# Gated linear attention by scores between all 256 tokens, without carried states

## The chip, the cores and the metric

The kernel runs on one core of a Trainium2 chip. The metric is the device time of one execution in microseconds (us); lower is better. TensorE (PE, with its weight loads listed as PEld), VectorE (DVE), ScalarE (ACT), GpSimd (POOL) and SyncE (SP, which issues nearly all transfers here) run side by side and wait for each other by semaphores. A difference of 0.3% of the time, some 3.6 us, is about the least that repeated runs tell from none.

## The reference, cut to what matters

One decoder layer for 256 tokens of width 1024: a modulation from a condition vector, one wide input projection whose columns feed all branches, a gated linear attention (GLA), a short convolution, gates and an output projection, and then a mixture of 64 experts. The part that changes is the attention:

```
def gla_chunked(q, k, v, log_a):                 # 4 heads, dk=128, dv=256, CHUNK=64
    b = jnp.cumsum(gc, axis=3)                   # within a chunk of 64 tokens
    q_t = qc * jnp.exp(b)
    k_t = kc * jnp.exp(-b)
    k_s = kc * jnp.exp(b_last - b)
    attn = jnp.where(causal, einsum(q_t, k_t), 0.0)
    o_intra = einsum(attn, vc)
    ...
    def step(state, inp):                        # over the 4 chunks
        o_i = q_i @ state
        state = d_i[..., None] * state + k_i.T @ v_i
```

After it each head's output is divided by its root mean square over the head's 256 values, scaled, and multiplied by silu(r).

## The kernel before, in words

The layer is done in two parts. The first part, up to about 300 us, works through 88 blocks of weights (`items`), 512 KB each, 24 matmuls or so a block. Blocks 0 to 15 are v and q/k, then come c (16 to 23), r (24 to 31), h (32 to 39), b, a, g, and the three output projections A, C and O. SP loads a block into a ring of 12 places; ACT rounds it to the short float format (`split_h`, L340), DVE forms the remainder (`split_l`, L347), which also frees the ring's place for the next load, and PE multiplies in three passes (`mm_blk`, L356). Splits run five blocks ahead of their matmuls (`LA`). Modulation weights come through the same ring, and DVE multiplies them with the condition (`mod_blk`, L257); the table `MODS` says beside which block each one stands.

The second part multiplies the experts' weights, 16 groups of 12 units of 2 MB each, with the tokens routed to them (L1020, L1048, L1075). `Stream` loads a unit whenever a piece of SBUF comes free; the first units are loaded while the first part still runs.

The order of the work is written by hand. The loop over blocks runs, for block `b`, first what is listed under `first(b, ..)`, then splits for a later block, then the evacuation of the block before, then `pre(b, ..)`, then the rest of the splits, then `at(b, ..)`, and then the block's matmuls. Each engine takes its own instructions in that order. The attention is such a list of steps between blocks 16 and 47:

- `gate0` to `gate8`: the forget gate, its sum over each chunk of 64 tokens (`bb`, the scan at L450), and the exponentials `eb`, `enb`, `ekb`.
- `k_evac`, `q_evac`: k and q leave PSUM times these exponentials, k twice (`ks` for the states, `kt_` for the scores).
- `gla_kst`, `gla_kst2` (block 27 and 28): `ks` transposed by PE (L481) and copied by ACT.
- `gla_attn`, `gla_attn2` (28 and 29): scores in two tiles of 128 by 128 tokens a head (L494), masked by DVE (L498) to two chunks each.
- `gla_state`, `gla_state2` (29 to 32): chunk by chunk k times v (L506, with 64 rows), and the running states S on ACT and DVE (L513, L515).
- `gla_o` (33 and 34): scores times v (L525) and states times q (L529), five matmuls for each of 8 halves of a head.
- `gla_ss` to `gla_ss4` (36 to 39): sums of squares by four column groups (L541), root, reciprocal, and the spread of each head's number to all 128 partitions by a matmul with a selection matrix `P1` (L556).

## Time and profile before

| | |
|---|---|
| median of 3 runs | 1206.16 us (1203.33 to 1206.17) |
| the profiled execution | 1202.4 us, of which the span from the first to the last instruction is 1200.5 us |
| PE / DVE / ACT busy | 903.8 / 381.6 / 224.6 us |
| moved by DMA | 477.84 MB, 398 GB/s over the span |

The span is read in stretches: "PE busy" is what PE did in one, "DMA share" is the mean busy share of the 16 DMA engines, and "PEclk" the clock that PE was granted, 1.00 being 2.4 GHz.

### The profile page before, as it was taken

Reading aid. Unit: us, or ns where it says so; the run is one execution under the profiler, and the core shown is the slowest. Engines: PE = TensorE matmul, PEld = TensorE weight load, DVE = VectorE, ACT = ScalarE, POOL = GpSimd, SP = SyncE. Lnnn points to the kernel's source line nnn. Section 1 sums busy time; section 2 is a strip of 40 time slices with the busy share of each in tenths; the row PEclk is TensorE's granted clock in tenths of the full one; section 3 lists DMA queues with packets and bytes.
Section 4 is the critical chain, followed back from the end, with each engine's and each line's share of the span. In section 5 each row is a group of like instructions: output and inputs, shape, how many; then the busy total and the mean of one; then the engine's idle time right before and its main releaser. Section 6 shows DMA issues by size and latency. Waiting matters only on the chain.

```text
span 1200.5 us, 14607 instructions
## 1 busy us (share of the span) xinstructions
PE 903.8 (75%) x6188; PEld 476.8 (40%) x6188; DVE 381.6 (32%) x720; ACT 224.6 (19%) x375; POOL 3.9 (0%) x15
## 2 busy tenths in 40 slices
PE   9999999999888766666666667676667566756575
PEld 6999999999342212121212212121212111412112
DVE  8968699664431111111111101020202000302103
ACT  6775545443210101010101000000000000100002
POOL 0000000000000000000000000000000000000000
PEclk9999999999998888798788888788888886989888
DMA  9987589979999999999999999999999999999996
GB/s 369 396 339 254 177 300 339 381 271 364 421 430 430 429 432 431 430 431 430 430 432 430 429 432 430 430 432 429 431 431 430 431 430 431 428 432 431 429 428 261
DMA packets 51483, 477.84 MB, mean 398 GB/s; under 512 B 5971, under 2 KB 6099, under 8 KB 27093
## 3 DMA queue, kind: packets, MB, share of 16 engines
q1 hardware_dynamic: 50544, 475.81, 95.8%
q8 instruction: 50, 0.82, 0.2%
q10 hardware_dynamic: 868, 1.05, 0.2%
q14 instruction: 21, 0.16, 0.0%
HBM read 475.79 MB, written 1.05 MB: 397 GB/s over the span
## 4 chain that ended last, share of the span: by engine, by line
DMA 67%; PE 28%; DVE 3%; ACT 0%; issue 0%; DVEq 0%; SPq 0%; ACTq 0%
DMA unit<-in_ew_dram 45%; DMA ring<-in_ew_dram 19%; PE z L356 17%; PE a L1048 3%; DMA unit<-in_el_dram 2%; PE m L364 2%; PE z L373 2%; PE m L1020 1%; PE m L1075 1%; PE m L529 0%; DMA xt<-in_xT_dram 0%; PE z L220 0%; PE m L506 0%; PE m L525 0%; PE m L312 0%
## 5 line engine op out<-in xcount | busy, mean ns | idle before, releaser
L1048 PE MATMUL a<-unit,xt 128*32 128x512 f32 x1440 | 209.5, 711 | 103.9 <-DMA unit<-in_ew_dram 103.9
L1048 PE MATMUL a<-unit,gt 128*32 128x512 f32 x736 | 121.7, 799 | 63.5 <-DMA unit<-in_ew_dram 59.9
L1048 PEld LDWEIGHTS a<-unit,xt 128*32 128x32 f32 x1440 | 43.8, 120 | 248.2 <-DMA unit<-in_ew_dram 139.0
L356 PE MATMUL z<-hhl,sp 128*128 128x256 f32 x1152 | 140.9, 284 | 0.0
L356 PEld LDWEIGHTS z<-hhl,sp 128*128 128x128 f32 x1152 | 138.9, 192 | 1.6 <-issue 1.5
L1024 ACT ACTIVATE xt<-m,modc,A 128x128 f32<-128x128 f32 x64 | 25.9, 453 | 518.5 <-PE m L1020 517.4
L347 DVE TENSOR_TENSOR sp<-ring,sp 128x1024 fp32r<-128x1024 f32 x88 | 106.8, 1219 | 40.2 <-ACT sp L340 40.1
L1048 PE MATMUL a<-ring,xt 128*32 128x512 f32 x608 | 84.2, 676 | 35.9 <-DMA ring<-in_ew_dram 35.9
L340 ACT CAST sp<-ring 128x1024 fp32r<-128x1024 f32 x88 | 91.5, 1048 | 93.8 <-PE z L356 66.6
L1079 DVE TENSOR_TENSOR wk<-wk,m 128x512 f32<-128x512 f32 (+2 forms) x64 | 41.7, 654 | 194.5 <-PE m L1075 194.5
L1066 DVE TENSOR_TENSOR xt<-a,xt 128x1024 f32<-128x1024 f32 (+3 forms) x19 | 20.0, 1054 | 257.4 <-PE a L1048 249.8
L1048 PEld LDWEIGHTS a<-unit,gt 128*32 128x32 f32 x736 | 24.3, 129 | 148.6 <-DMA unit<-in_ew_dram 93.1
L1075 PE MATMUL m<-xt,pwt 128*128 128x512 f32 (+2 forms) x136 | 64.5, 617 | 5.2 <-DVE xt L1066 5.2
L1056 DVE TENSOR_TENSOR gt<-gt,a 128x512 f32<-128x512 f32 x16 | 11.0, 687 | 173.8 <-ACT gt L1055 173.8
L1020 PEld LDWEIGHTS m<-scr,wk 128*128 128x128 f32 x512 | 58.7, 192 | 19.0 <-issue 18.7
L1020 PE MATMUL m<-scr,wk 128*128 128x128 f32 x512 | 62.4, 279 | 3.7 <-DVE scr L1009 2.9
L257 DVE SCALAR_TENSOR_TENSOR xt<-ring,xt 128x1024 f32<-128x1024 f32 x48 | 58.5, 1218 | 0.6 <-DMA ring<-in_modw_dram 0.2
L1048 PEld LDWEIGHTS a<-ring,xt 128*32 128x32 f32 x608 | 18.6, 117 | 97.3 <-DMA ring<-in_ew_dram 49.3
L1026 DVE TENSOR_SCALAR xt<-m,A,modc 128x128 f32<-128x128 f32 x64 | 23.3, 405 | 103.9 <-PE m L1020 103.9
L1048 PE MATMUL a<-ring,gt 128*32 128x512 f32 x208 | 36.3, 833 | 21.8 <-DMA ring<-in_ew_dram 21.1
L1075 PEld LDWEIGHTS m<-xt,pwt 128*128 128x128 f32 x136 | 26.0, 206 | 50.3 <-issue 38.0
L1055 ACT ACTIVATE gt<-a 128x512 f32<-128x512 f32 x16 | 9.6, 597 | 182.3 <-PE a L1048 182.3
(255 smaller groups left out, 633.0 us busy)
## 6 DMA issues: line engine op xcount, KB each, us to landing
unit<-in_ew_dram SPq DMA_DIRECT2D x136, 2048.0 KB, 38.8
ring<-in_ew_dram SPq DMA_DIRECT2D x48, 2048.0 KB, 38.8
ring<-in_win_dram SPq DMA_DIRECT2D x88, 512.0 KB, 7.8
ring<-in_modw_dram SPq DMA_DIRECT2D x48, 512.0 KB, 6.8
ring<-in_ew_dram SPq DMA_DIRECT2D x12, 512.0 KB, 7.3
unit<-in_el_dram SPq DMA_DIRECT2D x4, 1024.0 KB, 31.6
ring<-in_el_dram SPq DMA_DIRECT2D x4, 512.0 KB, 20.2
unit<-in_el_dram SPq DMA_DIRECT2D x4, 512.0 KB, 11.2
```

The lines of the kernel that those rows point to most:

```text
L257: V.scalar_tensor_tensor(scr, st.block("m", i, b), 1.0, cB, op0=OP.mult, op1=OP.mult, accum_out=modc[:, 4 * i + b:4 * i + b + 1])
L340: S.copy(sp(b)[:, 0], st.block("w", n, i))
L347: V.tensor_sub(t[:, 1], st.block("w", n, i), t[:, 0].bitcast(F32))
L356: T.matmul(ps, t[:, ws, k], rhs[rs][:, k], start=(clear and k == 0 and n == 0), stop=(k == KT - 1 and n == 2), skip_group_check=True)
L364: T.matmul(pb[:, h % 2], t[:, ws, h], hl[rs][:, kk], start=(kk == 0 and h % 2 == 0 and n == 0), stop=(kk == KT - 1 and h % 2 == 1 and n == ...
L373: T.matmul(pv[tt][hh], hl[rs][:, kk, 128 * tt:128 * tt + 128], t[:, ws, 512 * hh:512 * hh + 512], start=(kk == 0 and n == 0), stop=(kk == ...
L1020: T.matmul(ps[j], acc[:, tt, f:f + 128], Pm[:, tt], start=(tt == 0), stop=(tt == 1))
L1024: S.activation(xg[:, k], ps[j], AF.Identity, bias=B2[:, k:k + 1], scale=A2[:, k:k + 1])
L1026: V.tensor_scalar(xg[:, k], ps[j], A2[:, k:k + 1], B2[:, k:k + 1], op0=OP.mult, op1=OP.add)
L1048: T.matmul(ps[32 * j:32 * j + 32, 512 * hh:512 * hh + 512], lhsT[:, 32 * j:32 * j + 32], w[:, j, 512 * hh:512 * hh + 512], start=first, st ...
L1075: T.matmul(ps[:, :w], pwt[:, tt], X["y"][:, s], start=True, stop=True)
L1079: V.tensor_add(total[:, tt, s], total[:, tt, s], ps[:, :w])
```

## The change

The attention no longer carries states from chunk to chunk. The 256 tokens are taken as two tiles of 128. Inside a tile, the exponentials are measured from the end of the tile's first chunk: `wE` is the gate's sum at that end minus the running sum, and `eq` and `ek` get exponentials of plus and minus it (first chunk) and of the running sum (second chunk). One product of k and q then gives the scores of all pairs of a tile; the products of the first 64 tokens as keys are one matmul, those of the second 64 as keys, against the second 64 as queries alone, another (`gla_attn`, 64 rows of output each). For keys of tile 0 and queries of tile 1, `gla_far` multiplies k and q by the decay to the tile's edge, and a third product gives their scores. `gla_near` masks with a plain causal mask, `gla_cross` copies the third product, and `gla_o` needs two matmuls for each half of a head: 256 queries against the keys of tile 0, 128 against those of tile 1. Transposes, states and their copies are gone. The products stand at block 29, where those of the scores stood at block 28. The spread of the head norms takes one row of ones at partition 0, 32, 64 or 96 for each head, each into a PSUM tile of its own; `P1` is no longer filled at the start. Three entries of `MODS` move.

```diff
@@ -32,7 +32,7 @@
 FAR = 8192.0
 START = (2, 2, 0, 2, 8)
 XS = 38
-MODS = (16, 17, 18, 19, 22, 26, 27, 28, 31, 33, 34, 35, 37, 39, 41, 43, 45, 47, 49, 51, 52, 53, 54, 55, 56, 57, 58,
+MODS = (16, 17, 18, 19, 22, 26, 28, 29, 30, 33, 34, 35, 37, 39, 41, 43, 45, 47, 49, 51, 52, 53, 54, 55, 56, 57, 58,
         59, 60, 61, 62, 63)
 LA = 5
 SPLIT = ("T6", "T7", "T3")
@@ -229,7 +229,6 @@
     V.tensor_scalar(ident, jp, 0.0, None, op0=OP.is_equal)
     cmask = sm.tile([128, 128], I32, name="cmask")
     V.tensor_scalar(cmask, jp, 0.0, None, op0=OP.is_ge)
-    V.memset(cmask[0:64, 64:128], 0)
     tri = sm.tile([128, 128], BF, name="tri")
     V.tensor_scalar(tri, jp, 0.0, None, op0=OP.is_gt)
     trif = sm.tile([128, 128], BF, name="trif")
@@ -245,9 +244,6 @@
     G.memset(smask.rearrange("p (c t) -> p c t", t=64)[:, :, 0:1], 0.0)
 
     P1 = sm.tile([128, 2, TT, 128], F32, name="P1")
-    G.memset(P1, 0.0)
-    for h in range(H):
-        G.memset(P1[32 * h:32 * h + 1, h // 2, h % 2], 1.0)
     scr2 = sm.tile([128, 256], F32, name="scr2")
 
 
@@ -405,13 +401,19 @@
 
     t9 = big.tile([128, 4, 1024], F32, name="t9", tag="T9")
     gb = big.tile([128, 4, H, TOK], F32, name="gb", tag="T10")
-    la, bb, eb, enb = (t9[:, i].rearrange("p (h t) -> p h t", h=H) for i in range(4))
+    la, bb, eq, ek = (t9[:, i].rearrange("p (h t) -> p h t", h=H) for i in range(4))
     L["sr"], L["osq"] = (t9[:, 2 * i:2 * i + 2].rearrange("p a (k t) -> p (a k) t", t=TOK) for i in range(2))
     L["v"] = t8[:, 0].rearrange("p (t d) -> p t d", t=2)
     L["o"] = gb[:, 2:4].rearrange("p a h t -> p (a h) t")
-    ekb, qt, kt_, ks = (gb[:, i] for i in range(4))
-    decay = sm.tile([128, H, 4], F32, name="decay")
-    b4 = bb.rearrange("p h (c t) -> p (h c) t", t=64)
+    wE, qx, kx = gb[:, 0, 0:2].rearrange("p h t -> p (h t)"), gb[:, 1], gb[:, 3]
+    wE = wE.rearrange("p (a t) -> p a t", t=64)
+    kd, qd = (gb[:, 2].rearrange("p h t -> p (h t)")[:, 512 * i:512 * i + 512].rearrange("p (h t) -> p h t", h=H)
+              for i in range(2))
+    decay = sm.tile([128, 4, H], F32, name="decay")
+
+    def half(t, c):
+
+        return t.rearrange("p h (a c t) -> p (h a) c t", c=2, t=64)[:, :, c]
 
     def gate0():
         ps = zt(512)
@@ -450,84 +452,59 @@
         V.tensor_tensor_scan(fl(bb), smask, fl(la), 0.0, op0=OP.mult, op1=OP.add)
 
     def gate5():
-        S.activation(eb, bb, AF.Exp, scale=-1.0 / 16)
+
+        V.tensor_sub(wE, half(bb, 0)[:, :, 63:64].to_broadcast([128, 8, 64]), half(bb, 0))
 
     def gate6():
-        V.tensor_sub(ekb.rearrange("p h (c t) -> p (h c) t", t=64),
-                     b4[:, :, 63:64].to_broadcast([128, 16, 64]), b4)
-
-    def gate7():
-        V.tensor_copy(decay, eb.rearrange("p h (c t) -> p h c t", t=64)[:, :, :, 63])
-
-    def gate8():
-        S.activation(enb, bb, AF.Exp, scale=1.0 / 16)
-        S.activation(ekb, ekb, AF.Exp, scale=-1.0 / 16)
+        for d, sg in ((ek, -1.0), (eq, 1.0)):
+            S.activation(half(d, 0), wE, AF.Exp, scale=sg / 16)
+            S.activation(half(d, 1), half(bb, 1), AF.Exp, scale=-sg / 16)
+        for c in range(2):
+            S.activation(decay[:, c], bb[:, :, 64 * c + 127], AF.Exp, scale=-1.0 / 16)
 
 
 
     def gla_setup():
         g2 = big.tile([128, 4, 1024], F32, name="gc", tag="T11")
-        L["kst"] = g2[:, 0].rearrange("p (t d) -> p t d", t=2)
-        L["at"] = g2[:, 1].rearrange("p (t h i) -> p t h i", t=2, h=H)
-        for ch, i in ((1, 2), (2, 3), (3, 0)):
-            L["S", ch] = g2[:, i].rearrange("p (h d) -> p h d", h=H)
-        G.memset(g2[:, 1], 0.0)
-
-    def gla_kst():
-        L["pk"] = []
-        for tt in range(TT):
+        L["at0"] = g2[:, 0].rearrange("p (h i) -> p h i", h=H)
+        L["at1"] = g2[:, 1, 0:512].rearrange("p (h i) -> p h i", h=H)
+        G.memset(L["at0"][:, :, 0:128], 0.0)
+        G.memset(L["at1"], 0.0)
+
+    def gla_far():
+        for d, x, c, o in ((kd, kx, 0, 0), (qd, qx, 1, 128)):
+            V.tensor_mul(d, x[:, :, o:o + 128], decay[:, c, :, None].to_broadcast([128, H, 128]))
+
+    def gla_attn():
+        L["pa"] = []
+        a, b = slice(0, 128), slice(128, 256)
+        for k, q in ((kx[:, :, a], qx[:, :, a]), (kx[:, :, b], qx[:, :, b]), (kd, qd)):
             ps = mt(H, 128)
             for h in range(H):
-                T.transpose(ps[:, h], ks[:, h, 128 * tt:128 * tt + 128], ident)
-            L["pk"].append(ps)
-
-    def gla_kst2():
-        for tt in range(TT):
-            S.copy(L["kst"][:, tt], fl(L["pk"][tt]))
-
-    def gla_attn():
-        L["pa"] = []
-        for tt in range(TT):
-            s = slice(128 * tt, 128 * tt + 128)
-            ps = mt(H, 128)
-            for h in range(H):
-                T.matmul(ps[:, h], kt_[:, h, s], qt[:, h, s], start=True, stop=True)
+                if k is kd:
+                    T.matmul(ps[:, h], k[:, h], q[:, h], start=True, stop=True)
+                    continue
+                T.matmul(ps[0:64, h], k[:, h, 0:64], q[:, h], start=True, stop=True, skip_group_check=True)
+                T.matmul(ps[64:128, h, 64:128], k[:, h, 64:128], q[:, h, 64:128], start=True, stop=True,
+                         skip_group_check=True)
             L["pa"].append(ps)
 
-    def gla_attn2(tt):
-        V.copy_predicated(L["at"][:, tt], cmask[:, None, :].to_broadcast([128, H, 128]), L["pa"][tt])
-
-    def gla_state(*chs):
-        for ch in chs:
-            L["ps", ch] = [mt(2, 256) for _ in range(2)]
-        for h in range(H):
-            for ch in chs:
-                tt, r = ch // 2, slice(64 * (ch % 2), 64 * (ch % 2) + 64)
-                T.matmul(L["ps", ch][h // 2][:, h % 2], L["kst"][r, tt, 128 * h:128 * h + 128],
-                         L["v"][r, tt, 256 * h:256 * h + 256], start=True, stop=True)
-
-    def gla_state2(ch):
-        new = L["S", ch + 1]
-        for h in range(H):
-            if ch == 0:
-                S.copy(new[:, h], L["ps", ch][h // 2][:, h % 2])
-            else:
-                V.scalar_tensor_tensor(new[:, h], L["S", ch][:, h], decay[:, h, ch:ch + 1],
-                                       L["ps", ch][h // 2][:, h % 2], op0=OP.mult, op1=OP.add)
+    def gla_near(tt):
+        t, ps = (L["at0"][:, :, 0:128], L["at1"])[tt], L["pa"][tt]
+        for n, c in ((64, 0), (128, 64)):
+            V.copy_predicated(t[:n, :, c:c + 64], cmask[:n, None, c:c + 64].to_broadcast([n, H, 64]), ps[:n, :, c:c + 64])
+
+    def gla_cross():
+        S.copy(L["at0"][:, :, 128:256], L["pa"][2])
 
     def gla_o(h):
         ps = mt(2, TOK)
         vt = L["v"]
         for a in range(2):
             f = 256 * h + 128 * a
-            for tt in range(TT):
-                s = slice(128 * tt, 128 * tt + 128)
-                T.matmul(ps[:, a, s], vt[:, tt, f:f + 128], L["at"][:, tt, h],
-                         start=(a == 0 and tt == 0), stop=False, skip_group_check=True)
-            for ch in range(1, 4):
-                s = slice(64 * ch, 64 * ch + 64)
-                T.matmul(ps[:, a, s], L["S", ch][:, h, 128 * a:128 * a + 128], qt[:, h, s],
-                         start=False, stop=(a == 1 and ch == 3), skip_group_check=True)
+            T.matmul(ps[:, a], vt[:, 0, f:f + 128], L["at0"][:, h], start=(a == 0), stop=False, skip_group_check=True)
+            T.matmul(ps[:, a, 128:256], vt[:, 1, f:f + 128], L["at1"][:, h], start=False, stop=(a == 1),
+                     skip_group_check=True)
         L["po", h] = ps
 
     def gla_o2(h):
@@ -549,16 +526,15 @@
         V.reciprocal(scr2, scr2)
 
     def gla_ss4():
-        L["rso"] = []
+        L["rso"] = [mt(TOK) for _ in range(H)]
         for h in range(H):
-            if h % 2 == 0:
-                L["rso"].append(mt(2, TOK))
-            T.matmul(L["rso"][h // 2][:, h % 2], P1[:, h // 2, h % 2], scr2, start=True, stop=True)
+            r = slice(32 * h, 32 * h + 1)
+            T.matmul(L["rso"][h], onesf[r], scr2[r], start=True, stop=True)
 
     def o_norm(h):
         oT = L["o"]
         o = oT[:, 2 * h:2 * h + 2]
-        V.tensor_mul(o, o, L["rso"][h // 2][:, h % 2:h % 2 + 1].to_broadcast([128, 2, TOK]))
+        V.tensor_mul(o, o, L["rso"][h][:, None, :].to_broadcast([128, 2, TOK]))
         for k in (2 * h, 2 * h + 1):
             V.scalar_tensor_tensor(oT[:, k], oT[:, k], colt[:, CGG + k:CGG + k + 1], L["sr"][:, k],
                                    op0=OP.mult, op1=OP.mult)
@@ -611,25 +587,18 @@
     first(19, gate2)
     first(20, gate3)
     at(20, gate4)
-    at(21, gate6)
-    first(22, gate5)
-    first(23, gate8)
-    at(23, gate7)
+    at(21, gate5)
+    first(22, gate6)
     at(23, lambda: k_evac(0))
     at(24, lambda: k_evac(1))
     at(25, lambda: q_evac())
     at(25, gla_setup)
+    at(27, gla_far)
     at(40, st.free, "T12")
-    at(27, gla_kst)
-    at(28, gla_attn)
-    first(28, gla_kst2)
-    pre(29, gla_attn2, 0)
-    pre(29, gla_attn2, 1)
-    at(29, gla_state, 0, 1)
-    first(30, gla_state2, 0)
-    pre(30, gla_state2, 1)
-    at(31, gla_state, 2)
-    pre(32, gla_state2, 2)
+    at(29, gla_attn)
+    first(31, gla_cross)
+    pre(31, gla_near, 0)
+    pre(31, gla_near, 1)
     at(33, gla_o, 0)
     at(33, gla_o, 1)
     first(34, gla_o2, 0)
@@ -716,13 +685,12 @@
 
     def q_evac():
         for j in range(2):
-            V.scalar_tensor_tensor(qt[:, 2 * j:2 * j + 2], pq[j], 128.0 ** -0.5, eb[:, 2 * j:2 * j + 2],
+            V.scalar_tensor_tensor(qx[:, 2 * j:2 * j + 2], pq[j], 128.0 ** -0.5, eq[:, 2 * j:2 * j + 2],
                                    op0=OP.mult, op1=OP.mult)
 
     def k_evac(j):
         s = slice(2 * j, 2 * j + 2)
-        V.tensor_mul(ks[:, s], pk[j], ekb[:, s])
-        V.tensor_mul(kt_[:, s], pk[j], enb[:, s])
+        V.tensor_mul(kx[:, s], pk[j], ek[:, s])
 
     def b_evac(q, ps):
         if q == 0:
```

On PE, between blocks 26 and 34, stands before (L356 is the block's work, `gb` holds the scaled q and k, `gc` transposed k, scores and states, `t_126` v):

```order
L481 MATMUL m<-ident,gb 128x128 x8
L356 MATMUL z<-hhl,sp 128x256 x24
L494 MATMUL m<-gb 128x128 x8
L356 MATMUL z<-hhl,sp 128x256 x24
L506 MATMUL m<-t_126,gc 128x256 x8
L356 MATMUL z<-hhl,sp 128x256 x48
L506 MATMUL m<-t_126,gc 128x256 x4
L356 MATMUL z<-hhl,sp 128x256 x48
L525 MATMUL m<-gc,t_126 128x128 x2
L529 MATMUL m<-gb,gc 128x64 x3
```

And in the changed kernel, from the last pair of scores on (seven pairs like it stand ahead; L352 is the block's work there, `t_120` v):

```order
L487 MATMUL m<-gb 64x128
L488 MATMUL m<-gb 64x64
L485 MATMUL m<-gb 128x128 x4
L352 MATMUL z<-hhl,sp 128x256 x96
L505 MATMUL m<-gc,t_120 128x256
L506 MATMUL m<-gc,t_120 128x128
```

The transposes, both groups of state products and the three short matmuls of each half of a head have gone; all scores stand in one place, four blocks of work ahead of their use.

On DVE, from q's evacuation (L719) to the masks, stands before (`sp` are the split weights, `xt,modc` the modulation):

```order
L719 SCALAR_TENSOR_TENSOR gb<-m,t_181 128x512 x2
L347 TENSOR_TENSOR sp<-ring,sp 128x1024
L257 SCALAR_TENSOR_TENSOR xt,modc<-ring,xt 128x1024
L347 TENSOR_TENSOR sp<-ring,sp 128x1024
L257 SCALAR_TENSOR_TENSOR xt,modc<-ring,xt 128x1024
L347 TENSOR_TENSOR sp<-ring,sp 128x1024
L257 SCALAR_TENSOR_TENSOR xt,modc<-ring,xt 128x1024
L263 TENSOR_TENSOR modc<-modc,colt 128x4
L498 COPY_PREDICATED gc<-cmask,m 128x512 x2
```

And in the changed kernel (L688 is q's evacuation, L476 `gla_far`):

```order
L688 SCALAR_TENSOR_TENSOR gb<-m,t_175 128x512 x2
L343 TENSOR_TENSOR sp<-ring,sp 128x1024
L253 SCALAR_TENSOR_TENSOR xt,modc<-ring,xt 128x1024
L343 TENSOR_TENSOR sp<-ring,sp 128x1024
L476 TENSOR_TENSOR gb<-gb,decay 128x512 x2
L343 TENSOR_TENSOR sp<-ring,sp 128x1024
L253 SCALAR_TENSOR_TENSOR xt,modc<-ring,xt 128x1024
```

Behind q's evacuation now stand two splits and one modulation block, and then the two products that PE's third group of scores needs.

On ACT, at the exponentials, stands before (L453, L463 and L464 are the three exponentials, L715 copies c):

```order
L453 ACT_TABLE_LOAD
L453 ACTIVATE t_181<-t_181 128x1024
L340 CAST sp<-ring 128x1024
L715 COPY t_126<-z 128x512
L463 ACTIVATE t_181<-t_181 128x1024
L464 ACTIVATE gb<-gb 128x1024
L340 CAST sp<-ring 128x1024 x2
```

And in the changed kernel:

```order
L460 ACT_TABLE_LOAD
L460 ACTIVATE t_175<-gb 128x8x64
L461 ACTIVATE t_175<-t_175 128x8x64
L460 ACTIVATE t_175<-gb 128x8x64
L461 ACTIVATE t_175<-t_175 128x8x64
L463 ACTIVATE decay<-t_175 128x4 x2
L336 CAST sp<-ring 128x1024
L684 COPY t_120<-z 128x512
L336 CAST sp<-ring 128x1024 x2
```

All exponentials now stand ahead of the first of the three casts; before, two of the three stood behind it.

## Rows read from the trace of the kernel before

**Rows 1.** From the page: the span, and the chain of waits that ended last, as shares of the span by engine.

```profile
span 1200.5 us, 14607 instructions
...
DMA 67%; PE 28%; DVE 3%; ACT 0%; issue 0%; DVEq 0%; SPq 0%; ACTq 0%
```

**Rows 2.** Busy time by stretch: us from the span's start, its length, then busy us and instructions of PE, PEld, DVE, ACT and POOL, the granted clock of PE, the DMA share and GB/s.

```profile
94.60:149.70 55.10, 53.96 (x442) 51.24 (x441) 37.62 (x55) 26.18 (x39) 0.00 (x0) 1.00 0.66 211
149.70:240.00 90.30, 90.30 (x753) 90.27 (x752) 79.29 (x113) 42.77 (x51) 0.00 (x0) 1.00 0.92 339
...
300.00:374.00 74.00, 63.04 (x489) 26.74 (x491) 25.68 (x97) 15.36 (x36) 0.00 (x0) 0.95 1.00 425
374.00:1180.00 806.00, 533.95 (x3301) 164.18 (x3293) 116.69 (x255) 45.01 (x97) 0.00 (x0) 0.85 1.01 430
```

**Rows 3.** The same view in stretches of 5 us, three of those in which the DMA engines had gaps.

```profile
235.00:240.00 5.00, 5.00 (x44) 5.00 (x43) 2.65 (x3) 1.80 (x2) 0.00 (x0) 1.00 0.63 211
...
260.00:265.00 5.00, 5.00 (x44) 5.00 (x43) 2.44 (x5) 0.62 (x1) 0.00 (x0) 1.00 0.60 182
...
295.00:300.00 5.00, 4.95 (x22) 2.87 (x21) 4.00 (x25) 3.06 (x9) 0.00 (x0) 1.00 0.88 313
```

**Rows 4.** The chain of waits in order of time: start us, us, what ran or was waited for.

```profile
150.06 109.43 PE z L356 x912
...
368.88 5.38 PE a L1048 x32
374.28 37.96 DMA unit<-in_ew_dram
```

**Rows 5.** PE's timeline from the transposes to the spread of the norms: start us, us, engine, line, operation, out<-in, partitions and elements, count, and idle time before it. A float32 matmul leaves two records. The last end of a row is modelled, so that a step's time is read from start to start.

```profile
94.59 1.04 PE L481 MATMUL m<-ident,gb 128*128 128x128 f32 x8
95.38 3.11 PE L356 MATMUL z<-hhl,sp 128*128 128x256 f32 x24
98.33 1.95 PE L494 MATMUL m<-gb 128*128 128x128 f32 x16
100.04 3.11 PE L356 MATMUL z<-hhl,sp 128*128 128x256 f32 x24
103.08 0.70 PE L506 MATMUL m<-t,gc 64*128 64x256 f32 x2
104.86 1.99 PE L506 MATMUL m<-t,gc 64*128 64x256 f32 x14 [1.08 <-DVE gc L498]
106.78 6.02 PE L356 MATMUL z<-hhl,sp 128*128 128x256 f32 x48
112.73 1.99 PE L506 MATMUL m<-t,gc 64*128 64x256 f32 x8
114.65 6.01 PE L356 MATMUL z<-hhl,sp 128*128 128x256 f32 x48
120.50 0.61 PE L525 MATMUL m<-gc,t 128*128 128x128 f32 x4
...
124.88 3.12 PE L356 MATMUL z<-hhl,sp 128*128 128x256 f32 x24
127.84 0.61 PE L525 MATMUL m<-gc,t 128*128 128x128 f32 x4
...
132.22 3.00 PE L356 MATMUL z<-hhl,sp 128*128 128x256 f32 x23
...
138.15 1.07 PE L541 MATMUL m<-t,onesf 128*32 128x256 f32 x16
139.15 8.89 PE L356 MATMUL z<-hhl,sp 128*128 128x256 f32 x72
148.10 1.97 PE L556 MATMUL m<-scr,P 128*128 128x256 f32 x8
149.71 40.54 PE L356 MATMUL z<-hhl,sp 128*128 128x256 f32 x335
```

**Rows 6.** DVE's timeline, four of its rows between the scan and the masks, with the same columns.

```profile
84.27 1.22 DVE L456 TENSOR_TENSOR gb<-t 128x1024 f32<-128x1024 f32 x1
86.63 1.22 DVE L347 TENSOR_TENSOR sp<-ring,sp 128x1024 fp32r<-128x1024 f32 x1 [1.14 <-ACT sp L340]
...
95.85 1.28 DVE L719 SCALAR_TENSOR_TENSOR gb<-m,t 128x512 f32<-128x512 f32 x2
...
104.08 1.34 DVE L498 COPY_PREDICATED gc<-cmask,m 128x512 f32<-128x512 int32 x2
```

**Rows 7.** ACT's timeline at the exponentials, with the same columns.

```profile
83.31 1.28 ACT L453 ACT_TABLE_LOAD   x1 [3.43 <-DVE t L450]
84.60 1.06 ACT L453 ACTIVATE t<-t 128x1024 f32<-128x1024 f32 x1
85.57 1.03 ACT L340 CAST sp<-ring 128x1024 fp32r<-128x1024 f32 x1
86.50 0.58 ACT L715 COPY t<-z 128x512 f32<-128x512 f32 x1
```

**Rows 8.** Stretches of 5 us as in rows 3, here for PE's busy time and the granted clock behind it.

```profile
320.00:325.00 5.00, 2.89 (x28) 0.97 (x24) 3.33 (x18) 1.18 (x2) 0.00 (x0) 1.00 1.00 429
325.00:330.00 5.00, 2.70 (x24) 0.83 (x17) 4.60 (x16) 0.00 (x0) 0.00 (x0) 1.00 0.99 426
...
360.00:365.00 5.00, 5.00 (x36) 1.30 (x32) 0.00 (x0) 0.00 (x0) 0.00 (x0) 0.71 1.03 439
```

## The prediction

> **What bounds the kernel now.** I read the chain of waits first: by engine it is two thirds DMA and a quarter PE [rows 1]. In order of time the two do not mix. Up to 374.28 us the chain runs almost wholly over PE, one piece of it 912 matmul records long, and from there to the end it is unit loads one behind the other [rows 4]. The second view is the table of stretches [rows 2]: from 300 us on the DMA engines are full, 1.00 and 1.01 of their time at 425 to 430 GB/s, so that stretch takes as long as its bytes. Between 94.6 and 149.7 us PE is busy for 53.96 of 55.10 us and in the next stretch for all of 90.30, while DMA stands at 0.66 and 0.92. The third view is the fine one [rows 3]: at 235, at 260 and even at 295 us the DMA engines had gaps (0.63, 0.60, 0.88), with PE busy throughout. Loads wait there for buffers that the blocks of the first part free.
>
> So the end is the moment at which the stream of expert weights becomes continuous, about 300 us, plus a fixed number of bytes at a fixed rate. That moment is set by PE's first part. What PE saves between 94 and 150 us should move everything behind it forward by the same amount, unless DVE, ACT or the loads cannot follow.
>
> **The change part by part, on PE.** From start to start in PE's timeline [rows 5]:
> - transposes: 95.38 - 94.59 = 0.79 us, gone
> - two-tile scores: 100.04 - 98.33 = 1.71 us for 8 products, 0.214 each, replaced
> - states: 106.78 - 103.08 = 3.70 us, with a wait of 1.08 in it, and 114.65 - 112.73 = 1.92, gone
> - outputs: 124.88 - 120.50 and 132.22 - 127.84, 4.38 us each, replaced
> - sums of squares: 139.15 - 138.15 = 1.00 us, unchanged
> - spread of the norms: 149.71 - 148.10 = 1.61 us for four products of 256 columns, 0.40 each, replaced.
>
> Removed or replaced are 0.79 + 1.71 + 3.70 + 1.92 + 8.76 + 1.61 = 18.49 us.
>
> What comes instead:
> - Scores: eight pairs of 64-row products and four of 128 by 128. Whether the two of a pair run side by side the trace does not show for 64 columns of weights; it does for 32: the eight products of the sums of squares, in four column groups, took 1.00 us, where two turns of 0.40 would be 0.80, so side by side with a quarter on top. I take one turn per pair with that quarter, 8 x 0.214 x 1.25 = 2.1 us, and 4 x 0.214 = 0.9 for the rest: 3.0. Lower bound 2.6, without the quarter; upper bound 4.3, all twenty one after another at 0.214.
> - Outputs: eight times one product of 256 columns and one of 128, 8 x (0.40 + 0.214) = 4.9 us; I take 5.0 (4.8 to 5.6).
> - Spread: four products in four row groups. The row products of the states show such groups side by side: 14 records of alternating halves took 1.92 us (104.86 to 106.78), 0.14 each, where 8 records of one half alone took the same 1.92, 0.24 each. I take one turn of 0.40 with a quarter on top, 0.5 us (0.4 to 1.61, if they do not overlap).
>
> Together 8.5 us (7.8 to 11.5), so PE needs **10.0 us** less (7.0 to 10.7).
>
> A 64-column matmul by itself is where a rule has to be weighed. TensorEngine Tiling (Array Packing) of the Trainium skill, section Instruction Overhead, says that a matmul's cost does not fall below that of some 60 columns; by that rule the narrower product of a pair would cost half of the wider one, and a pair that does not overlap 0.32 us, eight of them 2.6 in place of 3.4, which would make the upper bound of the scores 3.5. No row here times such a product alone, and I keep 4.3.
>
> **What lies beside it: ACT, DVE, SP, POOL.** Four half exponentials and two tiny ones replace three full ones. The table load waited 3.43 us for the scan and can now stand in that idle time [rows 7]. The first exponential needs `wE`, half of L456's 1.22 us, which ended near 85.5 before [rows 6]. From about 85.0, four halves of L453's 1.06 and two tiny ones, which I put at 0.2 each, a third of the copy's 0.58 [rows 7], give 87.5, and the rounding that began at 85.57 begins there, 2 us late. Queued behind it is the copy of c, and DVE waits for the rounding with block 27's remainder, which ended at 87.85 [rows 6]; near 90 is still 4.5 us ahead of the block's matmuls, 94.6 in the new order. The two later exponentials are no longer in front of the next roundings, so this is caught up within three blocks. Cost zero; up to 1 us if the strided halves are slower than their size says.
>
> DVE loses half of L456, two of the four products of k, and eight state updates, and gains two far products of 512 columns at about 0.6 us. The wait that the change adds is PE's third group of scores behind these two. q's evacuation ended at 97.13 [rows 6]; two splits and a modulation block behind it at 1.2 us and the two products put the far operands at about 102. PE comes to the scores after blocks 27 and 28, at 94.6 + 2 x 2.95 = 100.5, and to the third group 2.1 us later, 102.6. The margin is half a microsecond to one: zero taken, up to 2 us lost. What would stand behind PE there is block 29 and all that follows. The masks, the same columns in four pieces, stand two blocks, 5.9 us, ahead of the outputs, which covers their 1.34 [rows 6] and the copy of the third product. The reciprocal ahead of the spread ends as before one block behind block 37; there nothing changes.
>
> In SP's queue one modulation load moves past two block loads; the ring's order still follows its use. POOL loses its fills of `P1` at the start, where no one waits for them. The loads of the stretch must now land in 45 us in place of 55: 211 GB/s become 258, below the 339 of the next stretch [rows 2].
>
> The sum stands against the profiled execution: 1202.4 - 10.0 = 1192.4 us. That execution lies 3.8 under the median of the runs, 1206.16, and I put the same difference there: **1196.2 us**.
>
> **The rivals.**
> 1. *The groups do not overlap.* Pairs and the four row groups run one after another: PE needs 4.3 + 5.0 + 1.6 = 10.9 and saves 7.6, so 1198.6 us. For it: no row has 64-column groups. Against it: the two kinds of groups in rows 5 that did overlap. With a wait for the far products of up to 2 us it is 1200.6.
> 2. *The gain is swallowed by the loads.* If the engines of DMA, not PE, already set the pace between 195 and 235 us, what PE gains before comes back as a wait there, and the time stays at 1206. For it: 0.92 of DMA time over that stretch [rows 2]. Against it: PE had no idle time in it, and the gaps at 235 and 260 us come after it [rows 3], so the backlog had been worked off.
> 3. *Slower: PE's clock falls.* The place is the third group of scores. If PE stands idle there, the clock of 2.4 GHz may be cut to 1.2. In the expert part the granted clock was 0.71 at 360 us [rows 8], after stretches with waits. At 1.2 GHz a microsecond of work takes two; from 10 us of work at that clock on, the kernel is slower than before, and if all the blocks to 139 us ran so, 37 us more would make 1233. Against it: at 320 to 330 us PE was busy for only 2.89 and 2.70 of 5 us and the clock stayed at 1.00 [rows 8], and the wait of 1.08 us at 104 us [rows 5] cost nothing either. TensorE: Matmul & The Clock Gate, in the Trainium skill, section HAM oscillation, warns of this pattern, thin groups of matmuls between waits; rows 8 show both outcomes.
>
> That the change doesn't do what it says could only be rival 1: everything else on PE is a count of instructions.
>
> **How the numbers follow.** Forecast 76%, rival 1 11%, rival 2 6%, rival 3 3%, and 4% for waits on DVE or ACT larger than bounded that eat most of the gain. The forecast's own range is a saving of 7 to 11.5 us, 1194.7 to 1199.2, with the spread of the runs before, 2.8 us below their upper end, 1192 to 1200. With rival 1 and its wait, the range is 1192 to 1201.5. About 0.3%, 3.6 us, is the least that is told from no change: the forecast and rival 1 are faster by more than that, together 87%; from rival 2 and the larger waits 8% fall within it; rival 3 and the rest, 5%, are slower.
>
> **What would show it.** Right: from the start of block 27 to the start of block 39 PE takes about 45 us where it took 55.1; the scores take 3 us, each pair of outputs 2.5, the spread 0.5; PE has no idle time ahead of the third group; the stretches of DMA at 430 GB/s begin about 10 us earlier, and the last load lands as much earlier. Scores above 4 us or a spread of 1.6 would say rival 1. An idle time ahead of the third group with DVE's far products as what ended it would say that my margin was wrong. PE idle with weights as the cause between 150 and 240 us would say rival 2, a clock below 1.00 before 300 us rival 3. A PE that saves its 10 us while the end stays would make the prediction wrong at its first step, that the stream of experts starts when PE lets it.

## The result, and the profile after

| | before | changed |
|---|---|---|
| median | 1204.91 us (1203.33 to 1206.17, 4 runs) | 1193.47 us (1193.05 to 1195.71, 4 runs) |
| the profiled execution | 1202.4 us, span 1200.5 | 1193.86 us, span 1191.8 |
| ratio of the times | | 0.9909, 95% interval 0.9889 to 0.993 |

The changed kernel is faster by 0.9%, some 11 us; the interval leaves no room for "no change". Predicted were 1196.2 us with a range of 1192.0 to 1201.5.

The page of the changed kernel has the same picture of the whole as [rows 1], with the span and the chain by engine:

```profile
span 1191.8 us, 14477 instructions
...
DMA 68%; PE 29%; DVE 2%; ACT 1%; issue 0%; DVEq 0%; SPq 0%; ACTq 0%
```

PE's timeline answers to [rows 5], with the same columns (L352 is the block's work, L487 and L488 the two products of a pair, L485 the third group, L505 the longer of the two output products, L518 the sums of squares, L532 the spread):

```profile
87.80 12.28 PE L352 MATMUL z<-hhl,sp 128*128 128x256 f32 x101
100.01 0.32 PE L487 MATMUL m<-gb 128*64 128x128 f32 x1
100.01 0.33 PE L488 MATMUL m<-gb 128*64 128x64 f32 x2
...
101.90 1.16 PE L485 MATMUL m<-gb 128*128 128x128 f32 x8
102.81 11.76 PE L352 MATMUL z<-hhl,sp 128*128 128x256 f32 x96
114.41 0.60 PE L505 MATMUL m<-gc,t 128*128 128x256 f32 x2
...
116.94 3.12 PE L352 MATMUL z<-hhl,sp 128*128 128x256 f32 x24
119.90 0.60 PE L505 MATMUL m<-gc,t 128*128 128x256 f32 x2
...
122.44 5.99 PE L352 MATMUL z<-hhl,sp 128*128 128x256 f32 x48
128.36 1.07 PE L518 MATMUL m<-t,onesf 128*32 128x256 f32 x16
129.36 8.89 PE L352 MATMUL z<-hhl,sp 128*128 128x256 f32 x72
138.31 0.71 PE L532 MATMUL m<-scr,onesf 1*128 1x256 f32 x8
138.96 11.30 PE L352 MATMUL z<-hhl,sp 128*128 128x256 f32 x92
```

The reader sees no idle time in brackets on any row, and reads the steps from start to start again: scores 102.81 - 100.01 = 2.80 us, outputs 2.53 and 2.54, sums of squares 1.00, spread 0.65.

The stretches, as in [rows 2] but shifted with the work:

```profile
94.60:139.50 44.90, 44.84 (x386) 42.89 (x385) 34.28 (x49) 23.39 (x32) 0.00 (x0) 1.00 0.79 269
139.50:230.00 90.50, 90.50 (x756) 90.50 (x755) 79.98 (x115) 43.58 (x52) 0.00 (x0) 1.00 0.92 341
...
364.00:1170.00 806.00, 531.03 (x3282) 164.11 (x3274) 116.77 (x255) 45.06 (x97) 0.00 (x0) 0.85 1.01 430
```

The stretch with the attention is 10 us shorter, and the loads in it run at 269 GB/s where they ran at 211. The stretch behind it and the stream of experts are as they were, only earlier.

Where the time went is best read from marks in the trace: the first matmul of block 16, the first one behind the spread (block 39), the first of the O blocks, the moments at which 300 and 10 of the 478 MB were still to be moved (packets summed up by their end), and the last instruction. All times in us, from the profiled execution of each kernel. The runs e1 to e12 are the experiments below; those without a median ran once.

| kernel | block 16 starts | 16 to 39 | 39 to O | 16 to 300 MB left | 10 MB left to the end | profiled | median |
|---|---|---|---|---|---|---|---|
| before | 61.10 | 88.61 | 118.47 | 431.08 | 34.67 | 1202.4 | 1204.91 |
| changed | 60.67 | 78.29 | 118.42 | 421.07 | 36.47 | 1193.86 | 1193.47 |
| e1 | 62.25 | 78.39 | 118.42 | 420.81 | 35.46 | 1194.12 | |
| e2 | 61.07 | 78.00 | 118.42 | 421.07 | 34.65 | 1192.34 | |
| e3 | 61.34 | 79.27 | 118.47 | 421.97 | 35.90 | 1194.91 | |
| e4 | 62.43 | 80.07 | 118.42 | 422.47 | 36.11 | 1196.73 | |
| e5 | 61.43 | 78.29 | 123.32 | 426.22 | 35.91 | 1199.16 | 1199.03 |
| e6 | 62.21 | 78.29 | 118.41 | 421.01 | 34.63 | 1193.53 | 1193.55 |
| e7 | 61.19 | 78.29 | 114.98 | 417.62 | 36.47 | 1190.87 | 1190.39 |
| e8 | 61.40 | 78.29 | 118.40 | 421.05 | 36.47 | 1194.47 | 1194.47 |
| e9 | 61.59 | 79.55 | 118.43 | 422.19 | 36.05 | 1195.6 | |
| e10 | 61.23 | 78.00 | 118.41 | 420.41 | 35.31 | 1192.59 | 1193.61 |
| e11 | 61.50 | 77.99 | 118.43 | 420.76 | 35.21 | 1193.09 | 1193.14 |
| e12 | 61.75 | 78.29 | 118.43 | 421.19 | 34.75 | 1193.26 | 1193.52 |

From before to changed, PE saved 88.61 - 78.29 = 10.32 us between blocks 16 and 39, and 10.01 of them are still there when 300 MB are left. The two ends, the start up to block 16 and the last 35 us, differ by 1 to 2 us between executions of one and the same kernel (changed and e12). The profiled executions before and after happened to differ there by -0.43 and +1.80. The way from the O blocks to the mark of 300 MB ("16 to 300 MB left" less the two columns ahead of it) is 224.0 to 224.7 us in every kernel, so that this mark tells differences to about 0.7 us.

### The profile page after: what moved, and what is told of

Its sections match the earlier page's. It is cut to its first block, busy times and chain, and to the rows that moved or that the text cites. A ratio compares the mean times of both kernels' runs of the same rounds, so it can differ in the third digit from the quotient of the medians.

```text
span 1191.8 us, 14477 instructions
## 1 busy us (share of the span) xinstructions
PE 893.3 (75%) x6132; PEld 468.8 (39%) x6132; DVE 377.2 (32%) x712; ACT 222.4 (19%) x373; POOL 2.8 (0%) x11
## 4 chain that ended last, share of the span: by engine, by line
DMA 68%; PE 29%; DVE 2%; ACT 1%; issue 0%; DVEq 0%; SPq 0%; ACTq 0%
DMA unit<-in_ew_dram 48%; DMA ring<-in_ew_dram 20%; PE z L352 17%; PE a L1016 3%; PE m L360 2%; PE z L369 2%; PE m L988 1%; PE m L1043 1%; PE a L1168 0%; PE z L220 0%; PE m L292 0%; PE m L505 0%; PE m L308 0%; ACT wk L1182 0%; PE m L654 0%
## 5 line engine op out<-in xcount | busy, mean ns | idle before, releaser
L1016 PE MATMUL a<-unit,xt 128*32 128x512 f32 x1440 | 205.9, 699 | 100.2 <-DMA unit<-in_ew_dram 100.0
L1016 PE MATMUL a<-unit,gt 128*32 128x512 f32 x736 | 119.8, 787 | 69.6 <-DMA unit<-in_ew_dram 66.0
L352 PE MATMUL z<-hhl,sp 128*128 128x256 f32 x1152 | 140.1, 284 | 0.0
L352 PEld LDWEIGHTS z<-hhl,sp 128*128 128x128 f32 x1152 | 138.7, 191 | 1.2 <-issue 1.2
L1016 PEld LDWEIGHTS a<-unit,xt 128*32 128x32 f32 x1440 | 43.2, 119 | 243.9 <-DMA unit<-in_ew_dram 134.7
L1016 PE MATMUL a<-ring,xt 128*32 128x512 f32 x608 | 88.9, 710 | 38.6 <-DMA ring<-in_ew_dram 38.6
L1016 PEld LDWEIGHTS a<-unit,gt 128*32 128x32 f32 x736 | 24.0, 128 | 151.6 <-DMA unit<-in_ew_dram 97.5
L1043 PE MATMUL m<-xt,pwt 128*128 128x512 f32 (+2 forms) x136 | 65.8, 627 | 5.2 <-DVE xt L1034 5.2
L1016 PEld LDWEIGHTS a<-ring,xt 128*32 128x32 f32 x608 | 19.2, 121 | 100.1 <-issue 50.9
L1016 PE MATMUL a<-ring,gt 128*32 128x512 f32 x208 | 35.0, 804 | 19.2 <-DMA ring<-in_ew_dram 18.5
L1043 PEld LDWEIGHTS m<-xt,pwt 128*128 128x128 f32 x136 | 26.6, 210 | 52.8 <-issue 40.5
```

The source lines that it names most:

```text
L352: T.matmul(ps, t[:, ws, k], rhs[rs][:, k], start=(clear and k == 0 and n == 0), stop=(k == KT - 1 and n == 2), skip_group_check=True)
L1016: T.matmul(ps[32 * j:32 * j + 32, 512 * hh:512 * hh + 512], lhsT[:, 32 * j:32 * j + 32], w[:, j, 512 * hh:512 * hh + 512], start=first, st ...
L1043: T.matmul(ps[:, :w], pwt[:, tt], X["y"][:, s], start=True, stop=True)
```

## The experiments

The theory is that of the prediction: the end follows PE's first part one for one, and PE saved what the counted products say. The rivals to be told apart are that the groups do not overlap, that the loads or DVE set the pace, and, new with the profile, that something was lost at the end.

**e1: the pairs taken apart.**

```diff
             for h in range(H):
                 ...
                 T.matmul(ps[0:64, h], k[:, h, 0:64], q[:, h], ...)
-                T.matmul(ps[64:128, h, 64:128], k[:, h, 64:128], q[:, h, 64:128], ...)
+            for h in range(H):
+                ...
+                T.matmul(ps[64:128, h, 64:128], k[:, h, 64:128], q[:, h, 64:128], ...)
```

> The changed kernel with the same 16 narrow score products in another order: in each tile of 128 tokens first the four whose output lies in rows 0 to 63, then the four for rows 64 to 127, so that neighbours use the same 64 columns of the array. Theory (the two of a pair run side by side, and that alone makes the scores cost 2.80 us): the 16 products take about 3.3 us in place of 1.9, the scores 4.2 in all, and block 39 starts about 1.4 us later (140.4 in place of 138.96). Rival (a narrow product is cheap by itself, its neighbour does not matter): the scores stay within 0.2 us of 2.80.

The scores took 104.48 - 101.59 = 2.89 us and block 39 started 0.1 us later, so what I expected of the theory did not happen; by the number alone it was the rival. PE's timeline shows why (L491 are the products for rows 64 to 127):

```profile
101.59 0.76 PE L487 MATMUL m<-gb 128*64 128x128 f32 x5
102.08 0.27 PE L491 MATMUL m<-gb 128*64 128x64 f32 x1
102.19 0.27 PE L487 MATMUL m<-gb 128*64 128x128 f32 x1
102.19 0.28 PE L491 MATMUL m<-gb 128*64 128x64 f32 x2
...
103.57 1.16 PE L485 MATMUL m<-gb 128*128 128x128 f32 x8
104.48 0.72 PE L352 MATMUL z<-hhl,sp 128*128 128x256 f32 x4
```

In the program all eight records of L487 for a tile stand ahead of the first L491. In the trace the first L491 starts at 102.08, ahead of the sixth L487 at 102.19, and from there both run side by side. So the order within a tile did not matter, and this run could not make the products run one after another; that the halves overlap it does show. The records of L487 start every 0.11 us, those that run alone and those beside L491: the products for the other half cost them nothing.

**e2 and e10: square products in place of the pairs.**

```diff
...
-                T.matmul(ps[0:64, h], k[:, h, 0:64], q[:, h], ...)
-                T.matmul(ps[64:128, h, 64:128], k[:, h, 64:128], q[:, h, 64:128], ...)
+                T.matmul(ps[:, h], k[:, h], q[:, h], start=True, stop=True)
```

> The changed kernel with one 128 by 128 product for each head and tile in place of each pair; the quarter that the mask never reads is computed too. Theory (a pair costs one turn of a 128-column product plus the switch of the array's division): 8 x 0.214 + 4 x 0.214 = 2.57 us for the scores in place of 2.80, so that the pairs saved nothing over it. Rival (the pairs are cheaper because they compute a quarter less): 3.0 us or more.

```profile
100.32 2.84 PE L484 MATMUL m<-gb 128*128 128x128 f32 x24
102.92 11.76 PE L352 MATMUL z<-hhl,sp 128*128 128x256 f32 x96
```

Twelve products, 2.60 us, and block 39 0.29 us earlier: the pairs save nothing over whole products, they cost 0.2. Timed on the chip of e12:

> The kernel with square score products once more, now timed. Theory: scores 2.60 us in place of 2.80, so 0.2 us less, which timing can't tell from the changed kernel beside it; rival (some other effect of the shorter list): more than 1 us.

1193.61 us against 1193.52 of the changed kernel there: the 0.2 us cannot be told by timing.

**e3: the old spread.** `P1` is also filled at the start again.

```diff
-            T.matmul(L["rso"][h], onesf[r], scr2[r], start=True, stop=True)
+            T.matmul(L["rso"][h], P1[:, h // 2, h % 2], scr2, start=True, stop=True)
```

> The changed kernel with the spread of the head norms as before, by the filled selection matrix over all 128 rows. Theory (four row groups side by side gave 1 us): the spread takes 1.6 us in place of 0.65, and block 40 and all behind it come 1.0 us later. Rival (it was the wait for the reciprocal that cost, not the products): the spread stays at 0.7 us.

```profile
139.00 1.97 PE L534 MATMUL m<-scr,P 128*128 128x256 f32 x8
140.61 1.67 PE L355 MATMUL z<-hhl,sp 128*128 128x256 f32 x11
```

1.61 us again, and block 39 comes 0.98 us later counted from block 16. The new spread is worth 1.0 us, and 0.90 of it is left at 300 MB. That it is the overlap of the four row groups, and not the single row, which makes it cheap is seen in the single records: in the changed kernel all eight start between 138.31 and 138.65 us, the first four within 0.02 us of each other, while in e3 one starts every 0.22 us. A product of one row by itself is no cheaper: with 512 columns in the expert part, one of a single row (L1114) starts a record every 0.43 us, as one of 128 rows does (L1043).

**e4: the scores one block earlier.**

```diff
-    at(29, gla_attn)
+    at(28, gla_attn)
```

> The changed kernel with the score products one block earlier, at block 28. Theory (the place was needed: the far operands were ready at 100.7 us, 1.2 us before PE came to the third group): PE comes to the third group near 98.9 and stands idle for about 1.8 us with DVE's far products as what ends it; block 39 starts about 1.8 us later, 140.7. Rival (the wait is made up, since the two groups ahead also wait less or DVE runs ahead): block 39 starts within 0.3 us of 138.96.

```profile
102.55 1.16 PE L485 MATMUL m<-gb 128*128 128x128 f32 x8 [1.70 <-DVE gb L476]
```

The wait is there, 1.70 us with the far products (L476) as what ended it, and block 39 comes 1.78 us later counted from block 16, hardly more than the wait; the granted clock stayed at 1.00 to 120 us. The place two blocks behind the old transposes is what keeps DVE's far products off the path.

**e5 and e6: a dose of 4.8 us on PE, in a block and among the experts.**

```diff
+    def dose(n):
+        ps = mt()
+        for _ in range(n):
+            T.matmul(ps, onesb, onesb[:, None, :].to_broadcast([128, 4, 128]), start=True, stop=True)
...
+    at(50, dose, 23)                 # e5
...
+            if g == 6 and u == 5:    # e6
+                dose(23)
```

> The changed kernel with 23 products of ones added on PE ahead of block 50, 23 x 0.213 = 4.9 us, whose result nobody reads. Theory (the end follows PE's first part one for one): block 87 starts 4.9 us later, the last load lands 4.9 us later, and the time is about 4.9 us above the changed kernel's 1193.5. Rival (DVE or the loads set the pace between 150 and 235 us): less than 2.5 us of it arrives at block 87, and the time rises by less than 2.5.

> The same 23 products, but in the expert part, in the first layer of group 6 of 16, where the unit loads follow each other without a gap. Theory (there the loads set the pace): the last load lands within 0.3 us of the changed kernel's, the time stays within the spread of runs. Rival (PE paces the whole kernel): the time rises by 4.9 us.

PE's rows of the dose in e5, and then of the one in e6:

```profile
171.48 5.14 PE L570 MATMUL m<-onesb 128*128 128x512 bf16 x23
176.27 8.97 PE L352 MATMUL z<-hhl,sp 128*128 128x256 f32 x72
```

```profile
628.37 5.14 PE L570 MATMUL m<-onesb 128*128 128x512 bf16 x23
```

In block 50 the dose took 176.27 - 171.48 = 4.79 us. Counted from block 39 the O blocks start 4.90 us later than in the changed kernel, counted from block 16 the mark of 300 MB comes 5.15 us later, and the median is 1199.03 - 1193.55 = 5.5 us above e6 on the same chip. Among the experts the same dose lies at 628 us, between the marks of 300 and of 10 MB (483 and 1157 us); from the one to the other took 673.7 us for 673.6 in the changed kernel, and the median, 1193.55, is the changed kernel's 1193.47 but for the spread. This is the prediction's first step, shown from both sides: 4.8 us more on PE at 171 us are paid one for one, the same at 628 us are hidden under the loads. Other places were tried only between 100 and 140 us, with smaller amounts (e3, e4, e9).

**e7: a pass less in 16 blocks.** One of the three passes is left out in blocks 40 to 55, so b and a are computed with less precision.

```diff
+        two = items[b][0] in ("b", "a")
...
             for n, (ws, rs) in enumerate(PASSES):
+                if two and n == 1:
+                    continue
```

> The changed kernel with one of the three passes left out in the 16 blocks of b and a (40 to 55), so part of the projection's precision is not computed: 16 x 8 x 0.12 = 15.4 us less on PE. Theory: PE sets the pace only until DVE's splits run out of their lead, which was 7.7 us at its least (block 53), so that some 8 us arrive at block 87 and the time falls by about 8 against the changed kernel, with idle PE between blocks 45 and 60 that splits end. Rival (PE paces to the end of the first part whatever it saves): 15 us arrive. Other rival (the loads pace there): under 3 us arrive, and what ends PE's idle time goes back to casts that wait for the ring's loads.

PE's waits by what ended them, us in total, times, longest; then a row of PE's timeline, and the stretch from 160 to 180 us:

```profile
PE z L355 <- DVE gb L702: 9.7, 4, 7.1
```

```profile
165.08 5.45 PE L355 MATMUL z<-hhl,sp 128*128 128x256 f32 x32 [7.12 <-DVE gb L702]
```

```profile
160.00:180.00 20.00, 13.10 (x94) 12.77 (x95) 19.93 (x28) 12.12 (x15) 0.00 (x0) 0.83 0.83 272
```

Of 15.4 us only 3.44 arrive at the O blocks, 3.45 at 300 MB, and 3.2 in the median (1190.39 against 1193.55). PE waits for DVE, as the theory had it, but not for the splits whose lead I had counted: L702 is `b_evac`, which empties the projection's PSUM tiles, in DVE's queue behind splits, modulation blocks and the attention's own normalisation (`o_norm`); DVE is busy for 19.93 of 20 us. Of the 12 us lost, 9.7 are these waits. Most of the rest is the clock, 0.83 in that stretch: 32 records took 5.45 us behind the idle 7.12, where they take 32 x 0.12 = 3.8 at full clock. So behind this change about 3.4 us could still be had from PE in blocks 40 to 55, saved as here; beyond that DVE set the pace there.

**e8, e11 and e12: the last 35 us.** In the changed kernel's profile the last first-layer unit (L1016) and the first second-layer products (L1168) ran at little more than half the clock. Here are the clock in two stretches and PE's rows of that profile, and then PE's rows of a second execution of the same kernel, e12 (L1043 is the product behind the last big load):

```profile
1160.00:1165.00 5.00, 3.37 (x17) 0.75 (x18) 0.69 (x1) 0.60 (x1) 0.00 (x0) 0.58 0.99 418
1165.00:1170.00 5.00, 4.27 (x20) 1.26 (x23) 0.00 (x0) 2.07 (x3) 0.00 (x0) 0.50 1.01 420
```

```profile
1160.21 3.13 PE L1016 MATMUL a<-unit,xt 128*32 128x512 f32 x16 [3.00 <-DMA unit<-in_ew_dram]
...
1166.60 5.81 PE L1168 MATMUL a<-unit,gt 128*32 128x512 f32 x32 [0.73 <-ACT gt L1028]
1173.24 1.98 PE L1043 MATMUL m<-xt,pwt 128*128 128x512 f32 x4 [0.82 <-DVE xt L1034]
```

```profile
1160.92 1.93 PE L1016 MATMUL a<-unit,xt 128*32 128x512 f32 x16 [1.29 <-DMA unit<-in_ew_dram]
...
1165.67 4.48 PE L1168 MATMUL a<-unit,gt 128*32 128x512 f32 x24 [0.73 <-ACT gt L1028]
1170.77 1.06 PE L1168 MATMUL a<-unit,gt 128*32 128x512 f32 x8 [0.61 <-DMA unit<-in_el_dram]
1172.65 1.98 PE L1043 MATMUL m<-xt,pwt 128*128 128x512 f32 x4 [0.81 <-DVE xt L1034]
```

e8 fills PE's waits in the last group's first layer with products of ones, e11 those of the second layer too, with square scores:

```diff
+            if g == last and 2 < u < KT:
+                dose(8 if u < KT - 1 else 5)         # e8 and e11
...
         last_mm(0, 512, w[:, f], 2 * u + f)
+        dose((0, 2, 6, 3)[2 * u + f])        # e11
```

> The changed kernel with products of ones added in the last expert group behind units 3 to 7, where PE waits for loads. In its profiled execution PE's granted clock fell to 0.58 and 0.50 between 1160 and 1170 us, and the last two layers took 3.13 and 5.81 us where the kernel before had 1.92 for the first. Theory (1.5 to 2 us of the gain were lost there, since PE's work behind the last loads is on the path): with the clock at 1.00 in that stretch the profiled end comes 1.5 to 3 us after less of the last load, and the median falls by 1 to 2.5 us to about 1191.5. Rival (the clock at the end costs nothing, the last small loads set the end): the time stays within 0.5 us of 1193.5. Other rival (the added products delay the units): it rises.

> Square score products, and products of ones in PE's waits of the last group up to the last loads (the run before filled the first layer's waits, and the clock then fell in the second layer's). Theory (a granted clock of 1.00 from 1150 us to the end takes about 1.5 us off the way from the last 10 MB to the end, 36.5 us in the changed kernel's and the earlier filled run's profile, 34.7 in the kernel before): 34.7 us there, and a median 1 to 1.5 us under the changed kernel's. Rival (the small last loads or the added products themselves hold the end): no less than the changed kernel.

> The changed kernel unaltered, on the chip of the two runs above, to compare them with: 1193 to 1194.5 us; its way from the last 10 MB to the end shows how far that differs from one execution to the next.

e8: from the last 10 MB to the end 36.47 us as before. The clock was 1.00 from 1140 to 1170 us and then fell, and the product there (L1048, the L1043 of the changed kernel) took 3.53 us for 1.98:

```profile
1170.00:1175.00 5.00, 3.75 (x11) 1.33 (x12) 1.26 (x2) 0.00 (x0) 0.00 (x0) 0.71 0.94 382
```

The median, 1194.47, is 0.9 above e6's on that chip, so that of the three expectations the one in which the time rises came nearest. e11 held 1.00 from 1140 to 1185 us, but the way was 35.21 us, and the median 1193.14 against 1193.52 of e12, which had 34.75 us without any filling. Its last piece of the second layer stood waiting for the load all the same:

```profile
1170.59 1.06 PE L1172 MATMUL a<-unit,gt 128*32 128x512 f32 x8 [1.39 <-DMA unit<-in_el_dram]
```

What the clock costs there is read from the last big load. Where PE waits for it, as in e11 and e12, the L1043 product starts 1.92 us behind its landing. In the changed kernel's profile the load landed at 1169.98 us and L1043 started at 1173.24, which is 3.26 behind: PE came late by 1.3 us. Six of the twelve profiles without filling are late in this way, by 0.7 to 1.3 us: changed, e3, e4, e5, e7 and e9, which have more than 35.8 us in the table. Their clock was 0.57 to 0.72 over the 12 us around the start of the second layer. In the other six, e12 and the kernel before among them, it was 0.84 to 0.97, and PE was not late. So this loss comes and goes between executions of one kernel. The rival of e8, that the clock at the end costs nothing, does not hold for the late ones; but in its own profile e8 lost as much on the next product, and what e11 saved is less than the timing tells.

**e9: a narrow product by itself.**

```diff
+        spare = mt(H, 128)
+        for n in range(8):
+            T.matmul(spare[0:64, n % 4, 64:128], kx[:, n % 4, 0:64], qx[:, n % 4, 0:64], ...)
```

> The changed kernel with eight more narrow products (64 columns of weights, 64 columns streamed) behind the third group of scores, all into rows 0 to 63 of a spare tile that nobody reads, so that none can run beside another. If a narrow product by itself costs as much as a wide one, as the 64-column matmuls of the states suggested (0.207 us each), they take 1.7 us and block 39 starts 1.7 us later; by the rule of a floor near 60 columns they take about half, 0.9 us. Taking the products in another order (the run before) had cost only 0.1 us, so the theory now is that each half of the array works through its own products: then the sixteen in pairs cost what the eight of the busier half cost, 8 x 0.214 = 1.7 us plus the start, whatever their order.

```profile
102.82 1.16 PE L485 MATMUL m<-gb 128*128 128x128 f32 x8
103.91 1.15 PE L493 MATMUL m<-gb 128*64 128x64 f32 x16
104.98 2.29 PE L352 MATMUL z<-hhl,sp 128*128 128x256 f32 x17
```

Eight in 1.07 us, 0.13 each, not 0.207, and block 39 1.26 us later; the rest is in the third group ahead, 1.09 us from start to start for 0.91 in the changed kernel. Of the two forecasts the lower one, 0.9 us, is the nearer. The products of the kernel before, by which the higher one was made, are those of the states with q (L529):

```profile
120.94 0.78 PE L529 MATMUL m<-gb,gc 128*128 128x64 f32 x6
121.56 0.66 PE L525 MATMUL m<-gc,t 128*128 128x128 f32 x4
```

Three took 0.62 us. They stream 64 columns as e9's do, but have 128 columns of weights where e9's have 64. The records of their weight loads differ too, 192 ns on average for L529 and 138 for e9's L493. That it is the loading which sets the 0.207 fits this, but it is argued, and no run separates it.

## Why the prediction was right, step by step

- *What sets the end.* Shown by e5 and e6, and by the change itself: 10.01 of the 10.32 us saved up to block 39 are there at 300 MB. The small amounts of e3, e4 and e9 agree as far as that mark tells: 0.98, 1.78 and 1.26 us more at block 39 became 0.90, 1.40 and 1.12.
- *PE's sum.* Forecast were 8.5 us for scores, outputs and spread, and a saving of 10.0. Measured are 2.80 + 5.07 + 0.65 = 8.52 and 18.49 - 8.52 = 9.97. That the sum is met to 0.03 us is partly luck: scores (3.0 forecast) came out 0.2 lower, outputs (5.0) and spread (0.5) together 0.2 higher. From the first matmul of block 27 (94.16) to that of block 39 (138.96) PE took 44.80 us, the forecast's "about 45". The twelve blocks between the steps took 35.28 us in place of 35.63, counted as the stretch less the steps. I had not counted that; that fewer steps interrupt them is a guess.
- *The upper bound of the scores.* It came from a narrow product at 0.214 us. e9 gives 0.13, so all twenty one after another would have been about 3.6, and rival 1 was priced too high. It did not come: the pairs overlap (e1), the four row groups too (e3). But the pairs were no gain either, since whole products take 0.2 us less (e2). TensorEngine Tiling (Array Packing) of the Trainium skill, section Instruction Overhead, gives a floor near 60 columns, and my estimate by it was half of 0.214. e9's 0.13 is nearer to that than to the price I took; L529, which also streams 64 columns, took 0.207 and does not follow it.
- *ACT.* The table load went into the idle time (79.47), the exponentials ran from 84.56, and the rounding began at 86.85; I had said 87.5. DVE then waited 3.39 us for it, and block 27's remainder ended at 89.15, 5.0 us ahead of its matmuls:

```profile
79.47 1.28 ACT L460 ACT_TABLE_LOAD   x1
84.56 0.63 ACT L460 ACTIVATE t<-gb 128x512 f32<-128x512 f32 x1 [3.81 <-DVE gb L456]
...
86.85 1.03 ACT L336 CAST sp<-ring 128x1024 fp32r<-128x1024 f32 x1
```

```profile
87.92 1.23 DVE L343 TENSOR_TENSOR sp<-ring,sp 128x1024 fp32r<-128x1024 f32 x1 [3.39 <-ACT sp L336]
...
99.42 1.28 DVE L476 TENSOR_TENSOR gb<-gb,decay 128x512 f32<-128x512 f32 x2
```

- *The added wait.* The far products ended at 99.42 + 1.28 = 100.70; PE came to the third group at 101.90. The margin was 1.2 us, I had said half to one.
- *The loads.* 269 GB/s for a forecast 258, and PE did not wait for them.
- *The number.* 1196.2 forecast, 1193.47 measured, 2.7 too high. The sum against the profiled execution gave 1192.4 us; it came out at 1193.86, where the last 35 us took 1.80 more than before, 1.3 of them for the clock. The step that was mis-sized is the last one: I added the 3.8 us by which the profiled execution lay under the median of three runs. A fourth run and two further comparisons put the kernel before at 1204.91, 1203.45 and 1204.57, so 1206.16 was at the upper edge of its spread. From 1204.91, the same 10.0 us would have given 1194.9. Between the medians lie 11.4 us, 11.1 on the chip of e12; the 1 us more than PE saved is within the spread of the runs and has no cause shown. The forecast's own range, 1194.7 to 1199.2, was missed on the low side, and only the 2.8 us added for the spread of the runs took the measured time in. Its lower end held a slip besides: the 11.5 us of saving in it is the upper bound of the cost; the most that the sum could save was 10.7, which gives 1195.5, and 1192.7 with the spread.
- *Rival 2* fell with the 10.01 us that are still there at 300 MB, and PE was busy for all of the 90.50 us behind the attention. e5, where a dose arrived whole, agrees. *Rival 3* had no place, since PE had no idle time ahead of the third group; in e4, which put 1.70 us there, the clock stayed at 1.00, while in e7 it was 0.50 in the 3 us behind an idle time of 7.12.

## What to carry to other kernels

Find the moment from which the loads run without a gap. Here work of PE ahead of it was paid in full and work behind it was free, and a dose of a few microseconds on either side shows which is which. A dose tells what an added microsecond costs, not that a saved one comes back: at block 50 the 4.8 us added arrived whole (e5), and of the 15.4 us saved in blocks 40 to 55 only 3.4 did (e7). Where a step is replaced, count its products by time from start to start, including the waits that go with it, and look for the next engine in the queue behind: here PE could still give some 3 us before DVE's evacuations held it. An offset between one profiled execution and the median of three runs can be mostly spread, as here (3.8 us before, -0.4 after), and should not be added in full.

## What the runs showed of the hardware

Products for the two halves of 64 output rows overlap without standing in pairs: in e1 a product for the upper half started at 102.08 us, before a record for the lower half that stands ahead of it in the program and started at 102.19. Sixteen of them in two halves took 1.89 us (100.01 to 101.90), eight whole 128 by 128 products 1.71 before [rows 5], so that splitting a square product for the sake of an unused quarter costs a little and brings nothing. A product of 64 columns of weights with 64 streamed took 0.13 us by itself (e9), one of 128 with 64 streamed 0.207 (L529). Four products of one row each, in four row groups, took 0.65 us, and 1.61 over all rows one after another (e3).
